# Three Newton steps instead of four in the inverse square roots of a two-layer encoder trunk

## The chip, the core and the metric

The kernel runs on one core of one Trainium2 chip. The metric is the device time of one execution in microseconds (us); lower is better. Three runs of the kernel before took 1381.34, 1382.67 and 1380.99 us, so the median is 1381.34 us. A profile of one further execution is quoted throughout; engines are named as it names them: PE (TensorE matrix products), PEld (its weight loads), DVE (VectorE), ACT (ScalarE), POOL (GpSimd, which here mostly issues transfers) and SP (which issues transfers).

## What is computed

The reference is a two-layer encoder on 512 tokens of width 1024, all in float32. Cut to what matters here:

```
for l in range(DEPTH):                      # DEPTH = 2
    h = rms_norm(x, attn_norm_g[l])         # 1/sqrt over each token's 1024 values
    qa, ka, va, qb, kb, vb, ga, gb = split(h @ w_in[l])
    qa, ka = rope(rms_norm(qa)), rope(rms_norm(ka))   # per head of 64: 8 and 2 heads
    ya = window_gqa(qa, ka, va, sink) @ w_proj_a[l]
    qb, kb = rms_norm(qb), rms_norm(kb)     # per head of 64: 8 and 8 heads
    yb = neighbourhood_attn(qb, kb, vb, rel_bias) @ w_proj_b[l]
    x = x + (sigmoid(ga) * ya + sigmoid(gb) * yb) @ w_out[l]
    h = rms_norm(x, ffn_norm_g[l])
    x = x + (silu(h @ w_gate[l]) * (h @ w_up[l])) @ w_down[l]
```

where `rms_norm(x, g) = x * rsqrt(mean(x * x) + 1e-6) * g`. The inverse square roots are the small part of this that the change touches: one per token for each of four norms, and one per token and head for the four projections that are normalised by head.

## The kernel before

Every operand of a large product is split into a rounded part and a remainder, and each product is made as three matmuls (`hi*hi`, `hi*lo`, `lo*hi`), of 512 columns in the projections and of 256 in most of the feed-forward part, where a seven-product scheme for 2x2 blocks is used. PE therefore has 8074 matmuls to issue. Making the two parts of activations and of many weights, adding, normalising, masking and emptying accumulators is the work of DVE and ACT; weights come by transfers that POOL and SP issue.

**One order for all.** The program is written out by a planner. It runs the kernel's Python once "dry", with a clock per engine and a cost for each operation (`cost`, L270; `clock`, L260), and records two things: each choice that hangs on those clocks (`Layout.choose`, L109), and the first and last use of each buffer, from which `Layout.pack` (L137) gives every buffer its place in two arenas. Then the same Python runs again with the choices as recorded. The main thread of the program is PE's stream of projection matmuls. Everything else is written as chains (Python generators) that give up control with a `Need` (L358): "go on when these tiles are ready by the planned clocks, and a bank of PSUM is free". After each unit of three matmuls `drive` (L411) lets all chains go on whose needs are met. So a transposition for the attention stands in PE's stream just behind the unit at which, by the planned clocks, DVE has made its input. Each engine then executes its instructions strictly in this order, and waits where an input isn't there.

**The inverse square root.** `rsqrt` (L832) takes a tile of 128 partitions and `w` columns, halves its bits as an integer, subtracts them from a magic constant (2 instructions on DVE), and then runs four Newton steps of three DVE instructions each: a TENSOR_TENSOR (y*y) and two SCALAR_TENSOR_TENSOR. Each reads what the one before wrote. It is called twelve times:

- by `Norm.chain` (L861), once for each of the four norms, with w = 4. Its result `rstd` is then turned on PE and copied to the buffer `rows`.
- by `head_scale` (L945), four times in each layer: for the queries of the window attention (`chain_q`, w = 32), for its keys (`chain_kv`, w = 8), and for the two halves of the neighbourhood attention (`chain_norm_b`, w = 32 each). Its result `hf` is multiplied onto the projection; for the first two of these the rotation (`rope`, L971) follows, and then the transpositions on PE (`k_parts`, L1038, and `q_parts`, L1022).

**What else the steps of the prediction name.** In `head` (L1104) each piece of a softmax is multiplied by the reciprocal of its denominator either on ACT or on DVE, whichever has the earlier planned clock (L1137). At the start of the feed-forward part, `chain_x` (L1530) makes the normalised activations and their split block by block, `Quad.chain` (L615) prepares the first weight block, whose last five remainders come by a transfer with accumulation (`low_by_transfer`, L582) through POOL's queue, `w_load` (L553) puts plain loads of `w_down` into the same queue, and `m_step` (L1632) issues 24 matmuls of 256 columns for each of the seven products, in the order 1, 5, 6, 2, 7, 3, 4. After product 6 DVE has to read its bank (`seed_c`, L1664, an addition into a new bank) before product 7 may add to that bank.

Of the kernel before, what the change touches and what calls it, by code (L numbers as in the profile page):

```python
# [16 lines left out]
ALU = mybir.AluOpType  # L17
# [192 lines left out]
def trunk(ctx: ExitStack, tc: tile.TileContext, a: dict, out: bass.AP, lay: Layout):  # L210
# [10 lines left out]
    def nm(s):  # L221
        uid[0] += 1
        return f"{s}_{uid[0]}"
# [30 lines left out]
    def small(w, dtype=F32):  # L254
        return sp.tile([P, w], dtype, tag=f"s{w}_{dtype}", name=nm("sm"), bufs=6)
# [81 lines left out]
    V = Engine(nc.vector, "dve")  # L337
# [493 lines left out]

    def rsqrt(dst, src, w):  # L832

        ki, y, t = small(32, I32), small(32), small(32)
        V.tensor_scalar(ki[:, :w], src.bitcast(I32), 1, None, ALU.logical_shift_right)
        V.tensor_tensor(y[:, :w].bitcast(I32), magic[:, :w], ki[:, :w], ALU.subtract)
        for it in range(4):
            V.tensor_tensor(t[:, :w], y[:, :w], y[:, :w], ALU.mult)
            V.scalar_tensor_tensor(t[:, :w], t[:, :w], -0.5, src, ALU.mult, ALU.mult)
            V.scalar_tensor_tensor(dst if it == 3 else y[:, :w], t[:, :w], 1.5, y[:, :w], ALU.add, ALU.mult)  # L840

    class Norm:

# [17 lines left out]
        def chain(self):  # L861

            yield Need(keys=[f"acc{self.i}"])
            yield Need("pe", [self.acc], [at_slots])
            at_slots.take()
            ps = at_bank()
            for b in range(NB):
                T.matmul(ps[:, b : b + 1], self.acc[:, P * b : P * b + P], ones[:, 0:1], start=True, stop=True)
            ms = small(32)
            V.tensor_scalar(ms[:, :NB], ps[:, :NB], 1.0 / D, EPS, ALU.mult, ALU.add)  # L870
            at_slots.give(clock["dve"])
            self.rst = cp.tile([P, NB], F32, tag="rstd", name=nm("rstd"), bufs=2)
            rsqrt(self.rst, ms[:, :NB], NB)
            done.add(f"rst{self.i}")
            yield Need("pe", [self.rst], [at_slots])
            at_slots.take()
            ps = at_bank()
            for b in range(NB):
                T.transpose(ps[:, P * b : P * b + P], self.rst[:, b : b + 1].to_broadcast([P, P]), ident)
            self.rows = buf([S])  # L880
            V.tensor_copy(self.rows, ps)
            at_slots.give(clock["dve"])
            done.add(f"rows{self.i}")
# [61 lines left out]
    def head_scale(raw, nh, rst, res):  # L945

        ss = small(32)
        for b in range(NB):
            yield Need("act", [raw[b]])
            sq = act()  # L950
            A.activation(sq[:, : nh * HD], raw[b], AF.Square)
            yield Need("dve", [sq])
            V.tensor_reduce(ss[:, b * nh : b * nh + nh], per_head(sq[:, : nh * HD]), AX.X, ALU.add)
        yield Need()
        w = NB * nh
        rb = rst.unsqueeze(2).to_broadcast([P, NB, nh])
        v = lambda t: t[:, :w].rearrange("p (b h) -> p b h", h=nh)
        t = small(32)
        V.tensor_tensor(v(t), v(ss), rb, ALU.mult)
        V.tensor_tensor(v(t), v(t), rb, ALU.mult)  # L960
        V.tensor_scalar(t[:, :w], t[:, :w], 1.0 / HD, EPS, ALU.mult, ALU.add)
        f = sp.tile([P, 32], F32, tag="hf", name=nm("hf"), bufs=4)
        rsqrt(f[:, :w], t[:, :w], w)
        V.tensor_tensor(v(f), v(f), rb, ALU.mult)
        res.append(f)
# [828 lines left out]
```

## Time and profile before

| | us |
|---|---|
| median of three runs | 1381.34 |
| the profiled execution, whole | 1382.42 |
| its span, first to last instruction | 1380.6 |
| DVE busy | 909.6 |
| ACT busy | 708.8 |
| POOL busy | 316.2 |

The span is what the profile's pages and views show; 1382.42 - 1380.6 = 1.8 us of the profiled execution lie around it. The granted clock of TensorE averaged 0.997 over the span. Times in views are us from the start of the span. A row of the timeline merges neighbours of one kind: start, duration, engine, line, operation, output<-input, shapes, count, and in brackets how long the engine was idle before and who ended that. A matmul's duration includes the time for which it lies in the pipeline beside the next one, so durations of matmuls overlap: the pace of PE is read from the starts. All instructions are recorded by one helper, so every row has the same line, L310, and rows are told apart by tile and shape: `sm` are the small tiles of `rsqrt`, `hf` and `rstd` its results, `mm` and `at` the two pools of PSUM banks, `arena` all larger buffers.

### The profile page before, as it was taken

To read this page: it belongs to the slowest core of one execution; us is meant where nothing else is said; L and a number is where in the kernel's file an instruction comes from. 1 tells how busy PE (TensorE), PEld (TensorE's weight loads), DVE (VectorE), ACT (ScalarE), POOL (GpSimd) and SP (SyncE) were. 2 spreads that over 40 slices of the span, in tenths; PEclk is the share of its full clock that TensorE was granted. 3 is DMA by queue.
4 is the path that set the end of the run, shared out by engine and by line. 5 is a ranking of instruction groups with operands and counts; after the bars stand their busy time and mean duration, and the time that the engine had idled before them with its cause. 6 is when DMAs were issued, how large, how long until landed. Compare 5 with 4: busy or idle time off the path is not lost.

```text
span 1380.6 us, 20976 instructions
## 1 busy us (share of the span) xinstructions
PE 1371.4 (99%) x8074; PEld 1215.7 (88%) x8074; DVE 909.6 (66%) x1700; ACT 708.8 (51%) x1174; POOL 316.2 (23%) x327
## 2 busy tenths in 40 slices
PE   8999999999999999999999999999999999999998
PEld 7888888888899999999888888888889999999997
DVE  5876878455966657575648668784568747575653
ACT  6477667534744333343545675684456434333441
POOL 4542222310311110111353422222012110111111
PEclk9999999999999999999999999999999999999999
DMA  8997888973766484734899978879439483655536
GB/s 215 180 176 136 165 154 155 180 190 104 151 152 153 111 195 91 183 93 92 170 192 191 167 136 156 165 138 233 120 93 214 104 214 93 153 121 124 132 67 153
DMA packets 192357, 207.48 MB, mean 150 GB/s; under 512 B 25584, under 2 KB 159136, under 8 KB 192256
## 3 DMA queue, kind: packets, MB, share of 16 engines
q0 software_dynamic: 132928, 141.54, 54.9%
q1 hardware_dynamic: 58832, 63.91, 16.1%
q8 instruction: 64, 1.05, 0.3%
q10 hardware_dynamic: 496, 0.67, 0.2%
q14 instruction: 37, 0.30, 0.1%
HBM read 193.51 MB, written 2.10 MB: 142 GB/s over the span
## 4 chain that ended last, share of the span: by engine, by line
PE 94%; DVE 2%; issue 1%; DMA 1%; POOL 1%; ACT 1%; SPq 0%; POOLq 0%; ACTq 0%; DVEq 0%
PE mm L310 72%; PE at L310 21%; DVE arena L310 1%; POOL arena L310 1%; DVE sm L310 1%; DMA arena<-in_w_in 1%; DMA arena<-in_x 1%; ACT arena L310 1%; ACT L310 0%; SPq L310 0%; DVE hf L310 0%; ACT trig L310 0%; ACT sm L310 0%; DVE den L310 0%; POOLq L310 0%
## 5 line engine op out<-in xcount | busy, mean ns | idle before, releaser
L310 PE MATMUL mm<-arena 128*128 128x512 f32 (+1 forms) x5568 | 1109.0, 355 | 0.2
L310 PEld LDWEIGHTS mm<-arena 128*128 128x128 f32 x5568 | 904.2, 190 | 131.4 <-issue 0.6
L310 ACT CAST arena<-arena 128x1024 fp32r<-128x1024 f32 (+2 forms) x277 | 234.6, 871 | 212.3 <-DVE arena L310 205.2
L310 DVE TENSOR_TENSOR arena<-arena,arena 128x1024 fp32r<-128x1024 f32 (+2 forms) x268 | 262.0, 993 | 48.3 <-ACT arena L310 44.3
L310 PE MATMUL at<-arena 128*128 128x256 f32 (+1 forms) x1964 | 285.0, 289 | 0.3 <-DVE negm L310 0.2
L310 ACT ACTIVATE arena<-arena 128x1024 fp32r<-128x1024 f32 (+3 forms) x252 | 207.0, 843 | 150.1 <-DMA arena<-in_w_down 63.9
L310 PEld LDWEIGHTS at<-arena 128*128 128x128 f32 x1964 | 261.7, 191 | 14.1 <-DVE negm L310 1.2
L310 DVE TENSOR_TENSOR arena<-arena,mm 128x512 f32<-128x512 f32 x144 | 98.7, 685 | 242.3 <-PE mm L310 240.7
L310 POOL DMA_DIRECT2D arena<-in_w_in x163 | 161.8, 1367 | 307.2 <-ACT arena L310 289.4
L310 POOL DMA_DIRECT2D arena<-in_w_down x96 | 99.2, 1230 | 508.9 <-ACT arena L310 310.6
L310 DVE TENSOR_TENSOR arena<-arena 128x1024 f32<-128x1024 f32 (+3 forms) x196 | 158.1, 823 | 2.3
L310 DVE TENSOR_TENSOR arena<-at,arena 128x512 fp32r<-128x512 f32 (+4 forms) x158 | 104.2, 660 | 31.6 <-ACT arena L310 22.6
L310 ACT CAST arena<-at 128x512 fp32r<-128x512 f32 (+2 forms) x116 | 64.3, 554 | 62.6 <-PE at L310 61.2
L310 ACT ACTIVATE arena<-arena,negm 128x256 f32<-128x256 f32 (+1 forms) x128 | 68.2, 533 | 18.7 <-DVE negm L310 16.9
L310 PE MATMUL at<-cst,arena 128*128 128x128 f32 x472 | 72.6, 276 | 4.0 <-DMA arena<-in_x 3.8
L310 PEld LDWEIGHTS at<-cst,arena 128*128 128x128 f32 x472 | 57.7, 141 | 13.4 <-DMA arena<-in_x 4.1
L310 DVE TENSOR_TENSOR arena<-mm,arena 128x512 f32<-128x512 f32 x72 | 49.1, 687 | 22.7 <-PE mm L310 22.3
L310 ACT COPY arena<-at 128x512 f32<-128x512 f32 (+1 forms) x72 | 41.3, 585 | 43.5 <-PE at L310 42.9
L310 DVE CUSTOM_DVE_ANT_0 arena<-at,cst,nsnk 128x256 f32<-128x256 f32 (+1 forms) x64 | 34.4, 548 | 33.4 <-PE at L310 32.6
L310 DVE CUSTOM_DVE_ANT_0 arena<-at,arena 128x256 f32<-128x256 f32 x64 | 26.4, 420 | 20.9 <-PE at L310 20.6
L310 POOL DMA_DIRECT2D arena<-in_w_up x8 | 8.2, 1028 | 122.4 <-PE mm L310 67.9
L310 ACT ACTIVATE arena<-arena,vec2T 128x512 fp32r<-128x512 f32 x16 | 11.6, 726 | 47.6 <-DVE arena L310 47.6
(75 smaller groups left out, 434.5 us busy)
## 6 DMA issues: line engine op xcount, KB each, us to landing
arena<-in_w_in POOLq DMA_DIRECT2D x99, 512.0 KB, 7.3
arena<-in_w_down POOLq DMA_DIRECT2D x80, 512.0 KB, 6.8
arena<-in_w_gate SPq DMA_DIRECT2D x20, 1024.0 KB
arena<-in_w_up SPq DMA_DIRECT2D x20, 1024.0 KB
arena<-in_w_in POOLq DMA_DIRECT2D x64, 256.0 KB, 6.6
arena<-in_w_proj_a POOLq DMA_DIRECT2D x16, 512.0 KB, 7.6
arena<-in_w_proj_b POOLq DMA_DIRECT2D x16, 512.0 KB, 7.0
arena<-in_w_out SPq DMA_DIRECT2D x16, 512.0 KB
```

Source lines behind the costliest of these rows:

```text
L310: f(*args, **kw)
```

## The change

One Newton step less. The iteration count goes from four to three, and the last of the three writes the destination.

```
     def rsqrt(dst, src, w):
 
+
         ki, y, t = small(32, I32), small(32), small(32)
         V.tensor_scalar(ki[:, :w], src.bitcast(I32), 1, None, ALU.logical_shift_right)
         V.tensor_tensor(y[:, :w].bitcast(I32), magic[:, :w], ki[:, :w], ALU.subtract)
-        for it in range(4):
+        for it in range(3):
             V.tensor_tensor(t[:, :w], y[:, :w], y[:, :w], ALU.mult)
             V.scalar_tensor_tensor(t[:, :w], t[:, :w], -0.5, src, ALU.mult, ALU.mult)
-            V.scalar_tensor_tensor(dst if it == 3 else y[:, :w], t[:, :w], 1.5, y[:, :w], ALU.add, ALU.mult)
+            V.scalar_tensor_tensor(dst if it == 2 else y[:, :w], t[:, :w], 1.5, y[:, :w], ALU.add, ALU.mult)
```

Twelve calls lose 36 DVE instructions. Because the planner's clock of DVE moves, so do its choices: of the softmax multiplications 8 go from ACT to DVE (on DVE there are then 72 of 256 columns, before 61, and 24 of 384, before 27; on ACT 24, before 35, and 8, before 5), and units of the attention change places on all engines. The counts of all other operations stay. Three places are shown.

The first is on DVE in layer 0, from the end of the queries' `rsqrt` (`hf`) to the first sums of the keys (`TENSOR_REDUCE` into `sm`). The rows before:

```order
L310 TENSOR_TENSOR hf_455<-hf_455,rstd_357 128x32
L310 TENSOR_TENSOR arena_72<-arena_72,hf_455 128x512
L310 TENSOR_TENSOR arena_72<-arena_72 128x8x32 x2
L310 TENSOR_TENSOR arena_72<-arena_72 128x512
L310 TENSOR_TENSOR arena_72<-mm_398,arena_72 128x8x8x8
L310 TENSOR_TENSOR arena_72<-arena_72 128x512
L310 TENSOR_TENSOR arena_72<-arena_72,hf_455 128x512
L310 TENSOR_TENSOR arena_72<-arena_72 128x8x32 x2
L310 TENSOR_TENSOR arena_72<-arena_72 128x512
L310 TENSOR_REDUCE sm_542<-arena_72 128x2 x4
```

and the same place now:

```order
L310 TENSOR_TENSOR hf_447<-hf_447,rstd_357 128x32
L310 TENSOR_TENSOR arena_72<-arena_72,hf_447 128x512
L310 TENSOR_TENSOR arena_72<-arena_72 128x8x32 x2
L310 TENSOR_TENSOR arena_72<-arena_72 128x512 x2
L310 TENSOR_TENSOR arena_72<-arena_72,hf_447 128x512
L310 TENSOR_TENSOR arena_72<-mm_401,arena_72 128x8x8x8
L310 TENSOR_TENSOR arena_72<-arena_72 128x8x32 x2
L310 TENSOR_TENSOR arena_72<-arena_72 128x512 x2
L310 TENSOR_TENSOR arena_72<-arena_72,hf_447 128x512
L310 TENSOR_REDUCE sm_539<-arena_72 128x2 x4
```

Two more operations of 512 columns of the queries' work now stand ahead of the keys: the second block's last addition, and the third block's normalisation.

The second is on PE, further on in layer 0: from the four transpositions of the rotated keys (`at_652`, now `at_647`) to the eight of the rotated queries (`at_722` and `at_729`, now `at_701` and `at_708`); the `mm` rows between are projection matmuls. Before:

```order
L310 MATMUL at_652<-cst,arena_72 128x128 x4
L310 MATMUL mm_512<-arena_73 128x512 x3
L310 MATMUL mm_513<-arena_73 128x512 x6
L310 MATMUL mm_514<-arena_73 128x512 x6
L310 MATMUL mm_511<-arena_73 128x512 x6
L310 MATMUL mm_512<-arena_73 128x512 x6
L310 MATMUL mm_513<-arena_73 128x512 x6
L310 MATMUL mm_514<-arena_73 128x512 x3
L310 MATMUL at_722<-cst,arena_72 128x128 x4
L310 MATMUL at_729<-cst,arena_72 128x128 x4
```

and now:

```order
L310 MATMUL at_647<-cst,arena_72 128x128 x4
L310 MATMUL mm_508<-arena_73 128x512 x3
L310 MATMUL mm_509<-arena_73 128x512 x6
L310 MATMUL mm_510<-arena_73 128x512 x6
L310 MATMUL mm_507<-arena_73 128x512 x6
L310 MATMUL mm_508<-arena_73 128x512 x6
L310 MATMUL at_701<-cst,arena_72 128x128 x4
L310 MATMUL at_708<-cst,arena_72 128x128 x4
```

The keys' transpositions stand where they stood in the stream of projection matmuls; the queries' come 27 matmuls behind them and no longer 36. In layer 1 the keys' come 3 matmuls earlier in that stream, the queries' 6.

The third is POOL's queue at the start of the feed-forward part; it reads alike in both layers. Here `arena_73<-arena_72` are the remainders of the first weight block (products 5, 6, 7, 3 and 4, in this order), and `in_w_down` plain loads and remainders of `w_down`. The piece of the difference:

```order
 L310 DMA arena_73<-in_w_up 128x4x256 x4
 L310 DMA arena_73<-arena_72 128x1024
-L310 DMA arena_73<-in_w_down 128x2x256
-L310 DMA arena_73<-arena_72 128x4x256 x2
-L310 DMA arena_73<-in_w_down 128x2x256
-L310 DMA arena_73<-arena_72 128x4x256 x2
+L310 DMA arena_73<-arena_72 128x4x256
+L310 DMA arena_73<-in_w_down 128x2x256 x2
+L310 DMA arena_73<-arena_72 128x4x256 x3
 L310 DMA arena_73<-in_w_down 128x2x256 x6
```

The remainder for product 6 moves ahead of the first `w_down` load, and that for product 7 behind the second.

More of the change, by code (lines that the diff above doesn't have):

```diff
@@ L836, in rsqrt @@
         V.tensor_tensor(y[:, :w].bitcast(I32), magic[:, :w], ki[:, :w], ALU.subtract)
-        for it in range(4):
+        for it in range(3):
             V.tensor_tensor(t[:, :w], y[:, :w], y[:, :w], ALU.mult)
             V.scalar_tensor_tensor(t[:, :w], t[:, :w], -0.5, src, ALU.mult, ALU.mult)
-            V.scalar_tensor_tensor(dst if it == 3 else y[:, :w], t[:, :w], 1.5, y[:, :w], ALU.add, ALU.mult)
+            V.scalar_tensor_tensor(dst if it == 2 else y[:, :w], t[:, :w], 1.5, y[:, :w], ALU.add, ALU.mult)
     class Norm:
```

## The prediction

> **What bounds the kernel now.** First I read the busy shares, then the chain that ended last, then who waited for whom, and last the timeline at the places where the change moves something.
>
> ```profile
> PE 1371.4 (99%) x8074; PEld 1215.7 (88%) x8074; DVE 909.6 (66%) x1700; ACT 708.8 (51%) x1174; POOL 316.2 (23%) x327
> ```
>
> PE is busy 99% of the span, DVE, from which the change takes work, 66%. Busy alone doesn't show that PE goes at its pace, so I take that from the chain that ended last (start, duration, what):
>
> ```profile
> 257.32 95.23 PE mm L310 x420
> ...
> 371.67 5.87 PE at L310 x48
> ```
>
> 420 matmuls of 512 columns take 95.23 us, 0.227 each, with no other engine in the chain; 48 of 256 columns take 5.87, 0.122 each. A place where matmuls follow each other at this pace has no room for a faster DVE. What is left is where PE waited; in the view of waits the rows of PE and its weight loads are these (us in total, times, longest):
>
> ```profile
> PEld at L310 <- DMA arena<-in_x: 4.1, 2, 2.5
> ...
> PEld at L310 <- DVE negm L310: 1.2, 4, 0.4
> ...
> PEld at L310 <- DVE arena L310: 0.9, 3, 0.4
> ```
>
> The largest is the first load of x, before any norm. For DVE PE waited 1.2 + 0.9 = 2.1 us in the whole execution: 1.2 for the row maxima of the softmax (negm), 0.9 for other tiles. So I take PE as the bound everywhere behind the first 10 us, and the question is what the change does to these few short waits.
>
> **The change part by part.** *What goes on DVE.* The instructions of a Newton step depend on each other, so a step costs the distance between two starts of its first instruction:
>
> ```profile
> 46.29 0.19 DVE L310 TENSOR_TENSOR sm<-sm 128x32 f32<-128x32 f32 x1
> ...
> 46.97 0.19 DVE L310 TENSOR_TENSOR sm<-sm 128x32 f32<-128x32 f32 x1
> ...
> 56.81 0.17 DVE L310 TENSOR_TENSOR sm<-sm 128x8 f32<-128x8 f32 x1
> ...
> 57.42 0.17 DVE L310 TENSOR_TENSOR sm<-sm 128x8 f32<-128x8 f32 x1
> ...
> 353.97 0.16 DVE L310 TENSOR_TENSOR sm<-sm 128x4 f32<-128x4 f32 x1
> ...
> 354.56 0.16 DVE L310 TENSOR_TENSOR sm<-sm 128x4 f32<-128x4 f32 x1
> ```
>
> That is 0.68 us with 32 columns, 0.61 with 8 and 0.59 with 4. Six, two and four calls: 6 x 0.68 + 2 x 0.61 + 4 x 0.59 = 7.7 us of DVE time. None of it is on PE.
>
> *What comes to DVE.* 8 softmax multiplications come from ACT:
>
> ```profile
> L310 DVE TENSOR_SCALAR arena<-arena,sm 128x256 f32<-128x256 f32 x61 | 20.5, 368 | 0.9
> ...
> L310 ACT ACTIVATE arena<-arena,sm 128x256 f32<-128x256 f32 x35 | 17.0, 507 | 7.5 <-DVE sm L310 7.4
> ...
> L310 DVE TENSOR_SCALAR arena<-arena,sm 128x384 f32<-128x384 f32 x27 | 10.9, 437 | 0.2
> ```
>
> 11 more of 0.368 and 3 fewer of 0.437 are 2.7 us of DVE, so on balance it is 5.0 us lighter; ACT is relieved of 8. I cost this at nothing: in the attention the projection matmuls between a head's steps hide it. Where that cover is gone, a piece costs PE at most its own 0.37 to 0.44 us.
>
> *Keys and queries of layer 0.* PE in rows one to three, where keys (63.48) and queries (72.46) are turned; then DVE: its wait for the sine tables, two operations of the kind that now stand ahead of the keys, and the end of the queries' rotation:
>
> ```profile
> 63.48 0.93 PE L310 MATMUL at<-cst,arena 128*128 128x128 f32 x4
> 64.17 8.46 PE L310 MATMUL mm<-arena 128*128 128x512 f32 x36
> 72.46 1.03 PE L310 MATMUL at<-cst,arena 128*128 128x128 f32 x8
> ...
> 40.68 1.71 DVE L310 SCALAR_TENSOR_TENSOR arena<-trig,gqa 128x128 f32<-128x128 f32 x8 [0.35 <-ACT trig L310]
> ...
> 51.84 0.68 DVE L310 TENSOR_TENSOR arena<-arena 128x512 f32<-128x512 f32 x1
> 52.44 0.68 DVE L310 TENSOR_TENSOR arena<-arena,hf 128x512 f32<-128x512 f32 x1
> 53.16 1.36 DVE L310 TENSOR_TENSOR arena<-arena 128x256 f32<-128x256 f32 x3
> ...
> 70.17 2.09 DVE L310 TENSOR_TENSOR arena<-arena 128x256 f32<-128x256 f32 x4
> ```
>
> The first norm's step (0.59) is lost here: at 40.68 DVE waits for ACT's tables, which don't come earlier. What reaches the keys is the queries' and the keys' own step, 0.68 + 0.61 = 1.29 us, and the two operations that now stand ahead of them take 0.60 + 0.72 = 1.32 (by the starts). So the keys are ready when they were; PE's short wait before them (one of the three for "DVE arena", at most 0.4) stays: 0. The queries' rotation has the same work in all, so it ends 1.29 earlier, at 72.26 - 1.29 = 70.97. But PE now comes 9 matmuls earlier, 9 x 0.230 (64.17 to 72.46 by 36) = 2.07: its fourth transposition, which takes the last block, stood at 72.46 + 3 x 0.10 = 72.76, and would stand at 70.69. A margin of 0.50 turns into a wait of 0.28 us, some 0.3 with the hand-over. Behind PE there everything waits. Bounds: 0, if DVE gains more than I count, and 0.9, if the first norm's step is all that the planner counted on and a wait for ACT adds as much again; I take **+0.3**, nearest to the rows.
>
> *Layer 1.* The same places, PE's queries first, then DVE's end of their rotation:
>
> ```profile
> 749.29 1.03 PE L310 MATMUL at<-cst,arena 128*128 128x128 f32 x8
> ...
> 747.30 2.09 DVE L310 TENSOR_TENSOR arena<-arena 128x256 f32<-128x256 f32 x4
> ```
>
> DVE ends 1.29 earlier, at 748.10; PE comes 6 matmuls, 1.38, earlier, its fourth at 749.59 - 1.38 = 748.21. The margin shrinks from 0.20 to 0.11: 0, with an upper bound of 0.3 as in layer 0.
>
> *Start of the feed-forward part.* PE at products 6, 2 and 7, DVE's addition after product 6, and the same for products 2 and 7 in layer 1; then the busy times of the stretch (window, length, PE, PEld, DVE, ACT, POOL, clock, DMA):
>
> ```profile
> 377.37 3.04 PE L310 MATMUL mm<-arena 128*128 128x256 f32 x24
> 380.25 3.04 PE L310 MATMUL at<-arena 128*128 128x256 f32 x24
> 383.40 11.63 PE L310 MATMUL mm<-arena 128*128 128x256 f32 x84
> ...
> 382.55 0.69 DVE L310 TENSOR_TENSOR mm<-mm,arena 128x512 f32<-128x512 f32 x1
> ...
> 1059.16 3.04 PE L310 MATMUL at<-arena 128*128 128x256 f32 x24
> 1062.29 11.64 PE L310 MATMUL mm<-arena 128*128 128x256 f32 x84
> ...
> 353.00:384.00 31.00, 30.89 (x186) 27.46 (x187) 29.66 (x48) 22.16 (x27) 11.45 (x11) 1.00 0.93 181
> ```
>
> 24 matmuls take 2.88 us (377.37 to 380.25), but product 7 starts 3.15 after product 2, 0.27 late, and 3.13 in layer 1, 0.25 late: it waits for DVE's addition, which ends at 383.24. DVE is busy 29.66 of these 31 us, from the norm's `rsqrt` to this addition almost without a break, so the step that goes (0.59) should bring the addition forward, and both waits should go: **-0.52**. Bounds: nothing, if DVE then waits for ACT instead; no more than 0.52, since the next matmul is bound by PE's pace.
>
> *POOL's queue there.* The remainder for product 7 stands behind one more plain load:
>
> ```profile
> 368.21 1.27 POOL L310 DMA_DIRECT2D arena<-arena  x1 [5.65 <-ACT arena L310]
> 368.97 1.25 POOL L310 DMA_DIRECT2D arena<-in_w_down  x1
> ...
> arena<-arena POOLq DMA_DIRECT2D x10, 512.0 KB, 7.0
> ```
>
> Issued at 368.21 + 1.25 and, counted from the end of its issue, landing 7.0 us later, it is there at 377.7; PE wants it at 383.40. 5.7 us of cover: 0.
>
> *Heads.* Units of the 32 heads change places by a few matmuls. The four waits for `negm` (1.2 us) are of this kind, and may all go or come twice as often: 0, with bounds of -1.2 and +1.2.
>
> The sum: 0.3 + 0 - 0.52 + 0 + 0 = -0.2 us on the profiled execution, 1382.4 to 1382.2; that execution was 1.1 us above the median of the three runs (1381.34), so the forecast is 1381.34 - 0.2 = **1381.1 us**.
>
> **The rivals.**
>
> *The saving reaches PE in full (faster).* If PE were paced by DVE wherever a norm is made, all of the 7.7 us would come off: 1373.7. For it: the stretch above, where DVE is as full as PE. Against it: 2.1 us of waits for DVE in the execution, which with the 0.52 bound any gain at about 2.6 us: 1378.7. A matmul stretch without any norm, in the same columns as above:
>
> ```profile
> 260.00:353.00 93.00, 93.00 (x416) 77.12 (x414) 51.01 (x69) 42.55 (x61) 11.47 (x11) 1.00 0.65 154
> ```
>
> Weight loads are busy 83% there (77.12 of 93), while matmuls follow each other every 0.227 us. [...] I leave this rival 3%.
>
> *The remainder for product 7 comes late (slower).* The `w_down` load that now stands ahead of it must wait until its buffer's old readers are done, and the buffers have been placed anew. POOL does wait so elsewhere:
>
> ```profile
> POOL arena L310 <- DVE arena L310: 175.0, 14, 27.0
> ```
>
> 14 waits of 12.5 us on average. A wait of up to 5.7 us is covered; beyond that each us is PE's, once per layer. At 12.5 it is 2 x 6.8 = 13.6 us: 1395. Against it: the load had no wait in the execution before (368.97, 0.76 behind its forerunner). With kindred cases, a weight late by a new place of its buffer, 5%.
>
> *The new order costs more than it gives (within 0.2%, but above before).* The queries' wait at 0.9, 0.3 in layer 1, 1.2 in the heads and no gain in the feed-forward part: +2.4, 1383.7. What speaks for it is that the planner moved PE forward by 2.07 us where DVE gains 1.29. 12% for a result above 1382.5.
>
> *The change doesn't do what it says.* What DVE is relieved of, the planner fills by a third with multiplications (2.7 of 7.7). This changes DVE's busy time, not the end; it is in the forecast.
>
> **How the numbers follow.** 0.2%, about 2.8 us, is what a measurement of this kernel can tell from no change. The forecast of no change by that measure has 92%: its small terms lie between -2.6 and +2.4, and don't reach it. Faster gets 3%, slower 5%. The range takes in the bounds of the small terms but for the ends at which all of them fall on one side, with the 0.7 us by which the three runs scatter: 1379.4 to 1383.4.
>
> **What would show it.** Right: about 5 us less DVE busy time; PE and its share unchanged; PE's chain with the same pieces; in the feed-forward start 24 matmuls in 2.88 us between products 2 and 7; a wait of PE for "DVE arena" at about 70.7 us, at the queries' fourth transposition. Wrong: any wait of PE above 1 us that wasn't there, above all for a transfer at products 7, 3 or 4; or a span below 1378.

## The result, and the profile after

The changed kernel takes **1390.33 us** (median of five runs, 1387.92 to 1392.46) against 1380.99 us for the kernel before in the same session (1380.64 to 1382.67): ratio over all runs 1.0064, 95% interval 1.0053 to 1.0075 (the two medians alone give 1.0068). It is slower by 9 us, where 1381.1 had been forecast with a range up to 1383.4.

The profiled execution took 1391.43 us, 9.0 more than the one of before. The busy row of its page:

```profile
PE 1374.5 (99%) x8074; PEld 1217.0 (88%) x8074; DVE 905.5 (65%) x1672; ACT 704.6 (51%) x1166; POOL 316.6 (23%) x327
```

DVE is lighter, as it should be, and PE still shows 99%: the share hides the loss, since 9 us are 0.65% of the span. The chain that ended last shows it better, by engine, before and after:

```profile
PE 94%; DVE 2%; issue 1%; DMA 1%; POOL 1%; ACT 1%; SPq 0%; POOLq 0%; ACTq 0%; DVEq 0%
```

```profile
PE 88%; DMA 4%; DVE 3%; issue 2%; ACT 1%; POOL 1%; SPq 0%; POOLq 0%; DVEq 0%
```

PE's share of the chain fell from 94 to 88%, and that of transfers rose from 1 to 4%. The view of waits (us in total, times, longest) names the transfers; of these rows only that for `DVE arena` was there before, with 0.9:

```profile
PEld mm L310 <- DMA arena<-in_w_down: 6.1, 2, 3.1
PE mm L310 <- DMA arena<-in_w_down: 5.2, 2, 2.7
...
PEld at L310 <- DVE arena L310: 3.1, 8, 0.8
...
PEld at L310 <- DMA arena<-arena: 2.2, 3, 1.2
```

Two waits, one per layer, for `in_w_down`. PE's timeline at both places (start, duration, count; idle time and its releaser in brackets):

```profile
383.39 6.39 PE L310 MATMUL mm<-arena 128*128 128x256 f32 x50
392.45 6.95 PE L310 MATMUL mm<-arena 128*128 128x512 f32 x34 [2.67 <-DMA arena<-in_w_down]
...
1068.51 6.39 PE L310 MATMUL mm<-arena 128*128 128x256 f32 x50
1077.48 2.75 PE L310 MATMUL mm<-arena 128*128 128x512 f32 x17 [2.58 <-DMA arena<-in_w_down]
```

The 50 matmuls are products 7 and 3 (24 each) and the first two of the first `w_down` product. The third one needs the remainder of the first `w_down` slab (a slab is a piece of a weight that is loaded and split as one), and that isn't there. By the starts (a step of 0.227 taken off) PE lost 2.84 and 2.75 us; such a loss is called a hole from here on. The chain goes back from 392.45 to the transfer:

```profile
377.67 14.73 DMA arena<-in_w_down
392.40 0.04 issue
392.45 6.95 PE mm L310 x34
```

So the remainder was issued at 377.67, a little earlier than before (378.13), but took 14.73 us to land. Before, it was the second of three in this row of POOL:

```profile
377.42 3.21 POOL L310 DMA_DIRECT2D arena<-in_w_down  x3
```

It took 9.63 and landed at 387.76. PE comes for it 6.22 us behind the start of product 7 (in the changed kernel 392.45 - 2.84 - 383.39), so before at 383.40 + 6.22 = 389.62: its cover, the time from landing to need, was 1.86 us, and 1.93 in layer 1. The next view is that of transfers by queue, from issue to landing of this remainder (packets, MB, share of the 16 engines; q0 is POOL's queue, q1 that of SP), before and after:

```profile
q0 software_dynamic: 1412, 1.38, 78.1%
q1 hardware_dynamic: 440, 0.87, 31.4%
```

```profile
q0 software_dynamic: 1709, 1.66, 64.0%
q1 hardware_dynamic: 1056, 2.10, 46.4%
```

In the changed kernel 1.23 MB more of SP's loads were moved in that time; at the stretch's own rate (3.76 MB in 14.73 us) they are, as an estimate, 4.8 us of the 5.1 by which the remainder took longer. Which loads these are, the timeline of SP tells (two loads of 1 MB are merged in a row where two are named; the second of `in_w_up` starts 0.37 before the row's end). Before, and after:

```profile
350.63 24.85 SPq L310 DMA_DIRECT2D arena<-in_w_up  x2
387.29 11.29 SPq L310 DMA_DIRECT2D arena<-in_w_gate  x2
```

```profile
339.98 37.37 SPq L310 DMA_DIRECT2D arena<-in_w_up  x2
379.60 0.37 SPq L310 DMA_DIRECT2D arena<-in_w_gate  x1
```

The first load of the second `w_gate` block starts at 379.60 and not at 387.29, and the last of `w_up` at 376.98 and not at 375.11. Against the issue of the remainder `w_up`'s load moved by 2.3 us in layer 0, from 3.0 to 0.7 ahead of it, and `w_gate`'s from 9.2 behind it, shortly before the landing, to 1.9 behind it: the bytes of both are now moved while the remainder is under way. The order of SP's transfers is what it was. What moved is the place of the buffers: SP issues a load when the last reader of its buffer's place is done, and the plan, made anew with a shorter DVE clock, gave that buffer a place whose last user is done at 379.1 by the planned clocks and no longer at 386.7 (layer 1: 1051.3, before 1059.0).

The third part of the loss stands behind the hole of layer 0. The stretches there (window, length, PE, PEld, DVE, ACT, POOL, clock, DMA share, GB/s):

```profile
393.00:394.00 1.00, 1.00 (x6) 0.89 (x5) 0.32 (x1) 0.00 (x0) 0.00 (x0) 0.78 0.20 37
394.00:395.00 1.00, 1.00 (x7) 1.00 (x6) 1.00 (x2) 0.00 (x0) 0.00 (x0) 0.50 0.00 0
...
396.00:397.00 1.00, 1.00 (x6) 1.00 (x6) 0.39 (x1) 1.00 (x2) 0.00 (x0) 0.51 0.00 0
397.00:398.00 1.00, 1.00 (x10) 1.00 (x9) 0.84 (x1) 0.11 (x1) 0.59 (x1) 1.00 0.00 0
```

For 3.41 us, 393.57 to 396.98, the granted clock is 0.50, though PE has work. The 34 matmuls of this row take 6.95 us; in run e6 below the same 34, behind a wait without such a stretch, take 5.44: 1.5 us lost. Layer 1 has no such stretch. The sum: 2.84 + 2.75 + 1.5 = 7.1 of the 9.0 us; some 1.9 are left for shorter waits in the attention, the larger of them 0.51 us at 51.5, 0.49 at 73.9 and 1.00 at 914.9, less the two waits for `seed_c` (0.52), which are gone.

### The profile page after: what moved, and what is told of

The parts are those of the page before. It is cut to its first block, busy times and chain, and to the rows that moved or that the text cites. A ratio compares the mean times of both kernels' runs of the same rounds, so it can differ in the third digit from the quotient of the medians.

```text
span 1389.6 us, 20943 instructions
## 1 busy us (share of the span) xinstructions
PE 1374.5 (99%) x8074; PEld 1217.0 (88%) x8074; DVE 905.5 (65%) x1672; ACT 704.6 (51%) x1166; POOL 316.6 (23%) x327
## 4 chain that ended last, share of the span: by engine, by line
PE 88%; DMA 4%; DVE 3%; issue 2%; ACT 1%; POOL 1%; SPq 0%; POOLq 0%; DVEq 0%
PE mm L310 69%; PE at L310 20%; DMA arena<-in_w_down 2%; DVE arena L310 2%; DMA arena<-arena 2%; ACT arena L310 1%; DVE sm L310 1%; POOL arena L310 1%; DMA arena<-in_x 1%; ACT L310 0%; SPq L310 0%; DVE hf L310 0%; DVE rstd L310 0%; ACT trig L310 0%; ACT sm L310 0%
## 5 line engine op out<-in xcount | busy, mean ns | idle before, releaser
L310 DVE TENSOR_TENSOR arena<-arena 128x1024 f32<-128x1024 f32 (+4 forms) x196 | 158.2, 824 | 2.3
```

Of the source, the lines that this page charges most:

```text
L310: f(*args, **kw)
```

## The experiments

Theory A is the one above: the new plan's places bring SP's loads forward, and they delay the remainder. "+" and "-" in the table are us behind and ahead of the issue of the first slab's remainder; the columns are SP's last `w_up` load, its first load of the next `w_gate` block, the remainder's time from issue to landing, and PE's hole. (e4, e11 and e12 hold the `w_gate` load back much further and are told in the text.)

| kernel, layer | w_up | w_gate | remainder | hole |
|---|---|---|---|---|
| before, 0 and 1 | -3.0, -3.7 | +9.2, +9.2 | 9.6, 9.6 | 0, 0 |
| changed | -0.7, -1.7 | +1.9, +1.9 | 14.7, 14.6 | 2.84, 2.75 |
| e1, old plan, 3 steps | -3.7, -3.8 | +9.6, +9.6 | 9.8, 9.6 | 0, 0 |
| e2, new plan, 4 steps | -1.7, -1.7 | +1.9, +1.9 | 13.3, 14.3 | 2.02, 2.96 |
| e3, changed, load held | -1.7, -1.7 | +11.2, +12.5 | 10.5, 11.8 | 0, 0 |
| e5, before, one buffer moved | -3.6, -3.8 | +4.6, +4.6 | 9.6, 9.2 | 0, 0 |
| e6, changed, layer 1 moved | -1.7, -1.7 | +1.9, +6.6 | 13.5, 11.7 | 1.65, 0 |
| e7, before, cost 0.077 | -2.9, -3.8 | +2.3, +9.8 | 12.4, 9.8 | 0.88, 0 |
| e8, changed, cost 0.076 | -1.3, -1.7 | +7.2, +9.5 | 12.8, 11.8 | 0.95, 0 |
| e9, heads only | -3.6, -3.6 | +9.2, +9.2 | 9.6, 9.7 | 0, 0 |
| e10, norms only | -1.4, -1.7 | +2.0, +1.9 | 16.5, 16.1 | 4.59, 4.22 |

### Plan and arithmetic taken apart (e1, e2)

```
-        for it in range(3):
+        steps_n = 4 if lay.dry else 3        # e1;  e2: 3 if lay.dry else 4
+        for it in range(steps_n):
...
```

`lay.dry` is true in the planner's dry run and false when the program is written out.

> The planner's dry pass counts four Newton steps, the program that is written out has three: the order of all instructions and every buffer's place are those of the kernel before, only the 36 DVE instructions are gone. Theory A (the loss comes from the new plan: other buffer places let SP's loads of w_gate start earlier and run beside the remainder of the first w_down slab): the PE waits for in_w_down of 2.84 and 2.75 us are absent, SP's w_gate load starts at about 387 us as before, and the time is 1380 to 1381.5 us, ratio to before 0.999 to 1.000 (the two waits for seed_c, 0.52 us, may go). Rival B (fewer steps themselves bring transfers forward into a collision, whatever the plan): the waits stay and the time is about 1390 us, ratio 1.006.

> The reverse: the dry pass counts three steps, four are written out. Order and buffer places are those of the changed kernel, the arithmetic is that of the kernel before. Theory A: the waits for in_w_down stay in both layers (2 to 4 us each), the time is 1389 to 1393 us, ratio 1.006 to 1.009, since DVE also has 7.7 us of work that the plan doesn't know of. Rival B: no wait for in_w_down, 1381 to 1383 us.

Measured: e1 1381.27 us, ratio 0.9999 (0.9990 to 1.0007); e2 1392.47, ratio 1.0090 (1.0076 to 1.0105). In e2 the wait is where it was, with all four steps in place:

```profile
383.90 6.39 PE L310 MATMUL mm<-arena 128*128 128x256 f32 x50
392.15 3.09 PE L310 MATMUL mm<-arena 128*128 128x512 f32 x20 [1.85 <-DMA arena<-in_w_down]
```

The loss belongs to the plan and not to the steps; the 36 instructions by themselves can't be told from nothing. The waits for `seed_c` did not follow the steps either: e1, three steps in the old order, still has them (0.26 us each), e2, four steps in the new order, hasn't.

### The load held back (e3, e4)

```
+    behind = first_down if q == 1 and w == "w_gate" else None
...
     def load(self):
+        if self.behind is not None and not lay.dry:
+            nc.sync.dma_start(vec[:, 0:1], lows[self.behind][:16, 0, 0:1].bitcast(F32))
...
```

`first_down` is the number of the layer's first `w_down` slab, `lows` holds the remainders: a tiny transfer on SP now reads that remainder, ahead of the `w_gate` load.

> The changed kernel with one tiny transfer more on SP in each layer, ahead of the load of the second 512 columns of w_gate, which reads the remainder of the first w_down slab, so that SP can't start that load before this remainder has landed. Theory A (the two transfers share the bandwidth): the remainder lands about 10 us after its issue, not 14.7; both waits for in_w_down go, and with them the stretch of 3.4 us at a granted clock of 0.5; 1383 to 1385.5 us, ratio 1.0015 to 1.003, what is left being the waits of PE in the attention (some 2 us). Rival C (the remainder is late by its place in POOL's queue or by its issue, not by SP's load): the waits stay, about 1390 us.

> Old order and buffer places with three steps, as in the first of these runs, and the hold of the third. Theory A: in the old plan that load starts at 387.29 us and the remainder lands at 387.76, so the hold delays it by about 0.5 us and does nothing else: within 0.5 us of the first run, 1380 to 1381.5 us. If the loads behind the held one then come too late, slower than the first run by the PE wait that this makes.

Measured: e3 1383.44 us, ratio 1.0013 (1.0005 to 1.0022); e4, which has e1's plan, 1381.30, ratio 1.0000 (0.9991 to 1.0009). SP in e3:

```profile
339.75 36.36 SPq L310 DMA_DIRECT2D arena<-in_w_up  x2
387.94 0.58 SPq L602 DMA_DIRECT2D vec<-arena  x1
388.62 9.68 SPq L310 DMA_DIRECT2D arena<-in_w_gate  x2
```

The tiny transfer starts when the remainder has landed (387.92), the load behind it. Both holes and the stretch at half clock are gone, and 1.9 us of the 9.3 are left (1383.44 against 1381.57 for the kernel before in that session), with the changed kernel's order and places. `w_up`'s load alone, still 1.7 us ahead of the remainder, costs 1 to 2 us of landing time, which the cover takes. In e4 I expected the load half a microsecond later; the hold let go only at 399.23, behind an instruction of DVE, so the load came 14 us later, and PE still had no new wait.

### One buffer moved (e5, e6)

```
+        for i, x in zip(self.second[::4], (16896, 14848)):   # e6: (0, 10240)
+            starts[i] = x or starts[i]
         self.starts = starts
```

`second` lists the buffers of the second blocks; `[::4]` picks the first load of `w_gate` in each layer, and 0 leaves a place as it is.

> The kernel before, four steps, its order untouched; only one buffer in each layer has another place, the one that takes the first half of the second w_gate load. Its last user before is done some 4.3 us earlier in layer 0 and 4.2 us earlier in layer 1 by the planned clocks, so the load should start at about 383 us (before: 387.29) and 1062 us (1066.21). Theory A: the load then meets the last 5 us of the remainder of the first w_down slab and stretches them by about half (14.7 instead of 9.6 us were measured where it met nearly all of them): landing at about 390.5 us, PE waits 0.5 to 1.5 us for in_w_down in each layer, time 1382.5 to 1384.5 us. If the place of this buffer doesn't matter: no such wait, 1381.5 us as before.

> The changed kernel, its order untouched; only in layer 1 the buffer of the first half of the second w_gate load has another place, whose last user is done 4.7 us later by the planned clocks (1056.0 against 1051.3). Theory A: the load starts at about 1069.4 us instead of 1064.72, the remainder lands about 12 us or less after its issue instead of 14.6, PE's wait for in_w_down in layer 1 falls from 2.75 us to at most 0.5; layer 0 keeps its wait of 2 to 3 us. Time 1386.5 to 1388.5 us, ratio about 1.004. If order or issue cause the wait: both stay, 1390 us.

Measured: e5 1381.69 us, ratio 1.0002 (0.9993 to 1.0011); e6 1385.09, ratio 1.0030 (1.0019 to 1.0042). e6 is as expected in layer 1, where the hole went from 2.75 to 0 and nothing but that buffer differs. Layer 0, untouched, had 1.65 and not 2 to 3, without a drop of the clock:

```profile
390.95 5.44 PE L313 MATMUL mm<-arena 128*128 128x512 f32 x34 [1.49 <-DMA arena<-in_w_down]
```

Its `w_up` load came 1.0 us earlier against the remainder than in the profile of the changed kernel, and the time is below the 1386.5 to 1388.5 that I had expected. e5 missed: the load did come early (+4.6), but the remainder took 9.6 and 9.2 us, as without it; only the next one grew, from 9.6 to 10.9 and 10.7. My rule that half of the overlap is added was wrong. By the table the `w_gate` load counts where it starts about 2 us behind the issue (2.8 us in e7 with `w_up` early), and doesn't at +4.6 with `w_up` early. How late `w_up` is counts too: in e8 below, with `w_up` only 1.3 us ahead, the remainder took 12.8 us though `w_gate` started at +7.2.

### No Newton step touched (e7), and three steps with another plan (e8)

```
-            return n * per + 0.075 + wait
+            return n * per + 0.077 + wait      # e7, on the kernel before; e8, on the changed one: 0.076
```

This is the time, in us, that the planner counts for an instruction of DVE.

> The kernel before with four steps; one constant of the planner's cost of a DVE instruction is 0.077 and not 0.075, which no instruction's work depends on. By the planned clocks the w_gate load's first buffer is then free at 380.2 us in layer 0 (before 386.7) and at 1059.9 in layer 1 (before 1059.0). Theory A: a wait of PE for in_w_down of 1.5 to 3 us in layer 0 and none over 0.5 in layer 1; with other small moves in the attention 1383 to 1386.5 us, although no Newton step is gone. Rival (the loss needs the missing steps): no such wait, within 1.5 us of before.

> The changed kernel, three steps; the same constant is 0.076. By the planned clocks that buffer is free at 384.4 us in layer 0 (in the changed kernel 379.1) and at 1058.9 in layer 1 (1051.3). Theory A: no wait for in_w_down in layer 1 and at most 1 us in layer 0, no stretch at a lower clock; 1381 to 1384.5 us, ratio 1.000 to 1.002. Rival (the missing steps make the loss): the waits of 2.8 us stay, about 1390 us.

Measured: e7 1381.99 us, ratio 1.0005 (0.9996 to 1.0014); e8 1381.36, ratio 1.0001 (0.9992 to 1.0010). e7 shows the wait in the kernel with four steps, in layer 0 alone, as its places foretold, though smaller than I expected, and the time, below my 1383 to 1386.5, can't be told from before:

```profile
389.84 5.44 PE L310 MATMUL mm<-arena 128*128 128x512 f32 x34 [0.71 <-DMA arena<-in_w_down]
```

In e8 the change costs nothing: a shift of 1 ns in a planned cost gives 9 us back. Both say the same: the loss goes with the places that the packer happens to give, and not with what is computed.

### Which calls bring the plan about (e9, e10)

```
-        for it in range(4):
+        ns_ = 4 if w == 4 else 3        # e9;  e10: 3 if w == 4 else 4
+        for it in range(ns_):
...
```

> Three steps in the eight inverse square roots by head, four in the four norms, planned and written so. By the planned clocks the first buffer of the second w_gate load is then free at 386.7 and 1059.0 us and that of the last w_up load before it at 371.4 and 1043.7, all as in the kernel before. Theory A, refined by the runs so far (the remainder is late only where the w_up load starts less than 2 us ahead of it and the w_gate load some 2 us behind it): no wait of PE for in_w_down, the two waits for seed_c of 0.26 us stay, the attention's units move: 1380.5 to 1383.5 us. Rival (any replanning with fewer steps costs it): about 1390 us.

> The reverse: three steps in the four norms, four by head. By the planned clocks those buffers are free at 379.1 and 1051.3 us (w_gate) and 373.5 and 1045.8 us (w_up), as in the changed kernel. Theory A: w_up's last load starts 0.7 to 1.8 us ahead of the remainder, w_gate's 1.9 us behind it, the remainder takes 13 to 15 us, PE waits 1.5 to 3 us for in_w_down in each layer: 1385 to 1390 us, ratio 1.003 to 1.006, so that four of the twelve calls make nearly the whole loss. Rival: the loss is spread over all calls, about a third of it here, no wait over 1 us.

Measured: e9 1382.88 us, ratio 1.0009 (1.0000 to 1.0018); e10 1395.72, ratio 1.0103 (1.0089 to 1.0117). e9 has no hole at `w_down`, and two short waits in layer 1 where the softmax's products are turned (the changed kernel has the same two; see "What comes to DVE" below):

```profile
759.03 0.44 PE L310 MATMUL at<-cst,arena 128*128 128x128 f32 x2 [0.30 <-DVE arena L310]
759.80 0.76 PE L310 MATMUL at<-cst,arena 128*128 128x128 f32 x2 [0.33 <-DVE arena L310]
```

e10 went beyond what I expected, since there the other half of the `w_gate` block was free as well and followed 2.3 us later:

```profile
349.60 25.67 SPq L310 DMA_DIRECT2D arena<-in_w_up  x2
378.24 2.64 SPq L310 DMA_DIRECT2D arena<-in_w_gate  x2
```

Three loads of 1 MB, 16.5 us for the remainder, holes of 4.59 and 4.22 us, and 10.2 us at half clock in all. One part of the change costs more (14.2 us) than the whole: each plan sets the places anew, and the parts don't add up.

### What a wait of PE costs (e11, e12)

On e4's kernel, with a row of small fills on POOL (`spin`, a tile of 64 columns that nothing reads) ahead of the remainder's issue:

```
             A.activation(lows[i], highs[i].bitcast(F32), AF.Copy, scale=-1.0)
+            if i in firsts and not lay.dry:
+                for _ in range((43, 50)[firsts.index(i)]):      # e12: (57, 76)
+                    nc.gpsimd.memset(spin, 0.0)
```

> What a wait of PE costs by itself: old plan with three steps and the w_gate load held behind the remainder, as in the fourth run, and in each layer a row of small fills on POOL ahead of the remainder's issue, 43 in layer 0 and 50 in layer 1, which should put it off by about 3.9 and 4.5 us, so that PE waits about 2.2 us in layer 0 and 2.8 us in layer 1. If the clock falls only behind waits longer than about 2.7 us (2.58 us of idle time left it, 2.67 didn't): no drop in layer 0, one of some 3.4 us at 0.5 in layer 1 or none, by a hair. If it hangs on the place (layer 0 of the changed kernel), the reverse.

> The same with 57 and 76 fills: waits of PE of about 3.5 us in layer 0 and 5.2 us in layer 1. If the clock falls behind waits longer than about 2.7 us: drops in both layers, each some 3.4 us at 0.5, and the length at 0.5 tells whether it grows with the wait; time about 1381 + 8.7 + 2 x 1.6 = 1393 us. If the drop in the changed kernel came from something else (the rate of transfers): none here, about 1390 us.

Measured, with two runs each: e11 1388.58 us, ratio 1.0048 (1.0030 to 1.0066); e12 1399.92, ratio 1.0130 (1.0112 to 1.0149). The fills took longer than I had reckoned (five or six start in each us in layer 1 of e11, from 1066 to 1069, where I had counted 0.09 us for each): holes of 2.07 and 3.59 us in e11, 5.02 and 9.10 in e12. The longer one of each, in layer 1 (first e11, then e12), and the stretches behind it:

```profile
1074.12 5.47 PE L310 MATMUL mm<-arena 128*128 128x512 f32 x34 [3.42 <-DMA arena<-in_w_down]
...
1070.00:1074.00 4.00, 0.69 (x4) 0.26 (x3) 1.00 (x1) 0.60 (x1) 2.97 (x3) 1.00 0.61 110
1074.00:1078.00 4.00, 3.88 (x28) 3.69 (x29) 1.82 (x2) 0.78 (x1) 0.00 (x0) 1.00 0.53 89
```

```profile
1083.78 6.56 PE L310 MATMUL mm<-arena 128*128 128x512 f32 x30 [8.93 <-DMA arena<-in_w_down]
...
1078.00:1084.00 6.00, 0.22 (x1) 0.22 (x2) 0.00 (x0) 0.00 (x0) 3.88 (x9) 0.51 0.45 72
1084.00:1088.00 4.00, 4.00 (x15) 3.61 (x16) 1.82 (x2) 0.25 (x1) 0.00 (x0) 0.50 0.52 91
```

With an idle time of 3.42 us the clock stayed at 1.00; with one of 8.93 it was at 0.50 for 10.24 us, from within the wait on, and with e12's other one, 4.85, for 6.83. The threshold of 2.7 us that I had expected doesn't show: 2.67 us came with a drop in the changed kernel, 3.42 in e11 with none. The rival that the drop came from the rate of transfers, by which e12 should have had none, is out.

## Why the prediction was wrong, point by point

**The bound.** Right: PE sets the time, DVE doesn't. e1 is the test: without the 36 instructions and with the old order the kernel takes what it took (1381.27 us, ratio 0.9999). The rival that all of the saving reaches PE is out.

**DVE's load.** 4.1 us less busy time, not 5.0. In e1 DVE is busy 903.9 us, 5.7 less: the 7.7 were taken from the distance between starts, while an instruction counts as busy for its 0.16 to 0.19 us. It changed nothing in the time.

**What comes to DVE.** Costed at nothing, with 0.37 to 0.44 for each piece that loses its cover. In one place of layer 1 the cover is gone: holes of 0.41 and 0.49 us in the changed kernel at 763.5 and 764.3. But no piece came from ACT there. DVE makes the same three multiplications before and after, PE has 9 matmuls ahead of the turnings and no longer 12, and the three take longer (before, then after):

```profile
759.11 1.33 DVE L310 TENSOR_SCALAR arena<-arena,sm 128x256 f32<-128x256 f32 x3
```

```profile
763.34 1.92 DVE L310 TENSOR_SCALAR arena<-arena,sm 128x256 f32<-128x256 f32 x3
```

Why they take longer stays open. e9, which has the same two holes, is 1.4 us slower than before.

**Keys and queries.** The +0.3 at 70.7 did not come. PE's row of the queries and DVE's end of their rotation in the changed kernel:

```profile
70.26 1.03 PE L310 MATMUL at<-cst,arena 128*128 128x128 f32 x8
...
68.56 1.75 DVE L310 TENSOR_TENSOR arena<-arena 128x256 f32<-128x256 f32 x3
```

PE comes about when I had it (72.46 - 2.07 = 70.39), but the rotation ends at 70.31 and not at 70.97: DVE gained more than I counted. It was within the bounds. Layer 1 came as forecast, without a wait at the queries.

**Start of the feed-forward part.** The two waits for `seed_c` went, -0.52 as forecast, but not for the reason given: by e1 and e2 they go with the new order, not with the step (from product 2 to product 7 it is 3.14 us in e1 and 2.88 in e2).

**POOL's queue: the step that failed.** I priced one transfer, the remainder for product 7, found 5.7 us of cover and wrote 0; for it that was right (it landed at 376.86). A later transfer in that very queue, the remainder of the first `w_down` slab, had 1.86 us in the trace of before, and I didn't work it out. And I took a landing time (7.0 us, a median) for a property of the transfer, though it depends on what SP moves beside it: for this remainder 9.6 us before, 14.7 and 14.6 now, and 4.2 to 4.3 in e11 and e12, where it goes alone. The rival "a weight late by a new place of its buffer" had the cause in one clause, but I looked at the buffer of the POOL load ahead of the late weight; it was the place of a buffer of SP, whose load got in its way. I gave it 5% because that POOL load had not waited before, and left SP out: the order of its transfers does not change. That says nothing here, since what moved was the time at which a buffer is free.

**Heads.** Costed at 0, with 1.2 us either way for the waits for `negm`. Those fell from 1.2 to 0.5 us, but waits of a kind that I had not listed came: for transfers between buffers, 0.49 and 1.00 us, and 0.51 for DVE at 51.5. e3, which has the new order without the collision, is 1.9 us slower than before, at 1383.44. So the rival "the new order costs more than it gives" (1383.7) is near in size to what the order does, by luck, since its terms were others; the forecast of 1381.1 would have been too low by some 2 us even with the transfer on time.

**The range.** It was built from terms of tenths of a microsecond on PE, DVE and ACT; none was there for transfers whose starts nobody plans. A new wait of PE above 1 us, above all for a transfer at products 7, 3 or 4, was named as what would show it wrong; such a wait came, right behind them, at the first `w_down` product.

What isn't settled: the waits of 0.5 to 1.0 us at 51.5, 73.9 and 914.9 are read from the trace and were not tried one by one, and why a load at +4.6 leaves the remainder alone while one at +1.9 costs 3 to 4 us was not tried by a run; the last section has what the traffic of the queues suggests. No version beats the kernel before by more than can be told: e1, e4 and e8 equal it.

## What to carry to other kernels

Where a planner or packer decides, a change has two effects, what it computes and what it makes the planner do; run the old plan with the new arithmetic before crediting or blaming the change. Before such a change, list every transfer's cover, not only those whose row in the queue moves: one with less cover than the scatter of its landing time (here 1.9 us against 9.2 to 16.5) is lost by chance. A load that is issued as soon as its buffer is free should be held behind the transfers that are due sooner; one tiny dependent transfer gave some 7 of 9 us back.

## What the runs showed of the hardware

**SP's loads and POOL's queue.** POOL had issued four transfers by 378.40 us, SP its two loads at 376.98 and 379.60, and they did not share evenly. In the changed kernel, from 380 to 382 us, the view of transfers by queue has one row:

```profile
q1 hardware_dynamic: 275, 0.56, 98.0%
```

For 2 us POOL's queue moved nothing. Before, it stood still as well, from 378 to 380 us (0.52 MB by SP's queue, 0.00 by POOL's), when the `w_up` load alone was under way. So in both kernels POOL's transfers stand still for about 2 us beside one such load; the changed one has this later in the remainder's time, and a second load behind it. In the 7 us behind the remainder's issue POOL's queue moved 0.42 MB in the changed kernel, 0.84 in e7 and 1.00 in e5. This suggests, and no run was made to test it, that the load at +4.6 in e5 did no harm because the remainder was nearly through when its bytes came.

**The granted clock at the waits for `in_w_down`.** It fell to 0.50 in the changed kernel (layer 0) and in e2 (layer 1), for 3.41 us each, in e10, for 6.83 us in layer 0 and 3.41 in layer 1, and in e12, for 6.83 and 10.24 us. PE's idle time alone doesn't sort these waits: 2.67 us in layer 0 of the changed kernel came with 3.41 us at 0.50, which cost 1.5 us more, while 2.58 us in its layer 1 and 3.42 in layer 1 of e11 came with the clock at 1.00 throughout. So these runs give no length of wait from which on the clock falls, and what else tells the two kinds apart was not tried by a run.
